# Hybrid pooling and gated-attention block on one core: last down chunk begun in PSUM, mean-square sums taken ahead, squares of the new x held until h2 is split, half of h2 split for all tokens at once

## The chip, the cores and the metric

The kernel runs on one core of a Trainium2 chip. The metric is the device time of one execution in microseconds (us), as the median of three executions. In the names below PE is the matrix engine, ACT the scalar engine, DVE the vector engine, POOL the GpSimd engine and SP the queue that issues most DMAs.

## The reference, cut to what matters

256 tokens of width 2048 go through two mixing branches and a gated feed-forward layer (FFN). The change touches the norms and the FFN; the two branches are left out here.

```python
mixed = (gates[:, :, 0] * y_a + gates[:, :, 1] * y_b) @ w_out[l]
x = x + rms_norm(mixed, norm_mix_post[l])
h = rms_norm(x, norm_ffn_pre[l])
f = (jax.nn.silu(h @ w_ffn_gate[l]) * (h @ w_ffn_up[l])) @ w_ffn_down[l]   # 2048 -> 5632 -> 2048
x = x + rms_norm(f, norm_ffn_post[l])

def rms_norm(x, g):
    y = x * lax.rsqrt(jnp.mean(x * x, axis=-1, keepdims=True) + EPS)
    return y * g
```

## The kernel before, in words

Every product is a job of 512 output columns. A job's weights come in steps of 128x1024 numbers: SP loads `raw` (3 buffers), ACT rounds it to `wh` (`high`, line 316), DVE takes the rest `wl = raw - wh` (`low`, line 320), with 4 buffers of each, and PE multiplies three times for every 128 rows k of the weight and each of the two token tiles t: hi by hi (line 347), hi by lo (348), lo by hi (349), each 128x512 into a bank of PSUM (`acc`). Jobs called fast do part of their rows with fewer products of blocks (class `Part`, lines 362 to 419); they are not changed.

The program is one list of units in the order in which PE is to multiply. `prepare_to` writes the weight work ahead of each unit, `soon` and `bg` hold other work that is put between units. A scheduler then fixes the order in which each engine's instructions stand; each engine goes through its own list in order and waits on semaphores.

Two places matter. The first lies between the last product of the mixing layer (`out`, 3) and the first product of the FFN (`gate`, 0). Its `done` functions call `out_done`: ACT squares the chunk of PSUM with a sum per row (line 821), DVE multiplies by the gain into `mg` (822). After the last chunk `first_residual` sums four partial sums (461), makes the mean plus epsilon (183), POOL raises it to the power -0.5 (185), and `residual_part` makes the new x in four chunks c for each t: `xr` (841). PE transposes it in 128x128 pieces into a bank `tr` (179), ACT writes the high half of h2 (218), DVE the low half (219). `h20h` is the high half of the rows k = 0 to 3 (chunk c = 0), `h21h` those of c = 1, and so on; the gate job takes k = 0 to 7 first for t = 0 (`head=4`), then for t = 1, and then the rest for both. Squares of the new x for the second norm (455) run on ACT between the splits, since all that work lies in one queue `bg`; the norm is needed only when the gate job ends (864).

The second place is the end: the jobs `down` (part, n) add a third of the FFN's rows each into `ff`, on the way out of PSUM (`down_done`, 894 and 896). The last job, (2, 3), does its last four steps for t = 0 and then for t = 1 (`tail=4`). After it come the add (896), the square on ACT (455), the gain (900), the mean (914), POOL's power (916), and `finish`: three chunks of the output on DVE (923) and the fourth by ACT and POOL (920, 921), all sent by SP (926).

Of the kernel before, what the change touches and what calls it, by code (L numbers as in the profile page):

```python
# [100 lines left out]
def tile_hybrid_block(ctx: ExitStack, tc: tile.TileContext, *aps):  # L101
# [79 lines left out]
    def rstd_of(ss, n, width, tag):  # L181
        m = st.tile([P, width], F32, tag="ms", name=nm("ms"))
        dve.tensor_scalar(m, ss, 1.0 / n, EPS, op0=ALU.mult, op1=ALU.add)
        r = one.tile([P, width], F32, tag=tag, name=nm(tag))
        pool.tensor_tensor(r, m, mhalf[:, :width], op=ALU.pow)
        return r
# [72 lines left out]
    class Job:  # L259
# [4 lines left out]
        def __init__(self, w, at, kt, width, fast, lhs, done, across=False, head=0, tail=0):  # L264
            self.w, self.at, self.lhs, self.kt, self.width, self.done = w, at, lhs, kt, width, done
            self.across, self.groups, self.ps, self.extra, self.fast = across, kt // GK, None, None, fast
            both = tuple(range(NT))
# [28 lines left out]
    class Step:  # L296
# [25 lines left out]
        def multiply(self, ts):  # L322
            j, g, hi, lo = self.j, self.g, self.hi, self.lo
            if j.ps is None:
                j.ps = [acc.tile([P, CW], F32, tag="acc", name=nm("acc")) for _ in range(NT)]
                if j.width > CW:
                    j.extra = [bank() for _ in range(NT)]
            for i in range(GK):
                k = g * GK + i
                first, last = k == 0, k == j.kt - 1  # L330
# [9 lines left out]
                for t in ts:  # L340
                    ah, al = j.lhs().get(k, t)
                    out = [(j.ps[t], slice(0, CW))]
                    if j.extra:
                        w = j.width // 2
                        out = [(ps[:, :w], slice(n * w, n * w + w)) for n, ps in enumerate((j.ps[t], j.extra[t]))]
                    for ps, cs in out:
                        pe.matmul(ps, ah, hi[:, i, cs], start=first, stop=False, skip_group_check=j.fast)  # L347
                        pe.matmul(ps, ah, lo[:, i, cs], start=False, stop=False, skip_group_check=j.fast)  # L348
                        pe.matmul(ps, al, hi[:, i, cs], start=False, stop=last, skip_group_check=j.fast)  # L349
# [102 lines left out]
    def squares(src, part, ts, cs):  # L452
        for t in ts:
            for c in cs:
                act.activation(scratch(), src[t][:, c * CW:(c + 1) * CW], AF.Square, accum_out=part[:, t, c:c + 1])

    def total(part, ts, tag):

        w = len(ts)
        ss = st.tile([P, w], F32, tag="ss", name=nm("ss"))  # L460
        dve.tensor_reduce(ss, part[:, ts[0]:ts[0] + w, :], axis=mybir.AxisListType.X, op=ALU.add)
        return rstd_of(ss, D, w, tag)
# [10 lines left out]
    def first_rstd():  # L473
        r = total(part0, (0, 1), "rstd0")
# [227 lines left out]
    def gla_out(h, t, v):  # L702
# [9 lines left out]
        act.activation(scratch(), ps, AF.Square, accum_out=ss)  # L712
        m = st.tile([P, 1], F32, tag="mso", name=nm("mso"))
        r = st.tile([P, 1], F32, tag="rso", name=nm("rso"))
        dve.tensor_scalar(m, ss, 1.0 / DV, EPS, op0=ALU.mult, op1=ALU.add)
        pool.tensor_tensor(r, m, mhalf[:, :1], op=ALU.pow)
# [94 lines left out]
    def out_done(n):  # L811
        def done(j, ts):
# [3 lines left out]
            for t in ts:  # L816
# [4 lines left out]
                act.activation(scratch(), j.ps[t], AF.Square, accum_out=part1[:, t, n:n + 1])  # L821
                dve.tensor_tensor(mg[t][:, c], j.ps[t], bcs[n], op=ALU.mult)
                if n == 3:
                    first_residual(t)
        return done

    def first_residual(t):
        r = total(part1, (t,), f"rstd1{t}")
# [10 lines left out]
    def residual_part(t, c, r):  # L839
        s = slice(c * CW, (c + 1) * CW)  # L840
        dve.scalar_tensor_tensor(xr[t][:, s], mg[t][:, s], r, xr[t][:, s], op0=ALU.mult, op1=ALU.add)
        ps = bank()
        for i in range(4):
            k = c * 4 + i
            v = ps[:, i * P:(i + 1) * P]
            transpose(v, xr[t][:, k * P:(k + 1) * P])
            h2["h"].split(c, (slice(None), i, slice(t * P, (t + 1) * P)), v, scale=column("ffn", k))

    def second_rstd():
        r = total(part2, (0, 1), "rstd2")  # L850
# [5 lines left out]
    fg = {}  # L856
# [28 lines left out]
    def down_done(part, n):  # L885
        def done(j, ts):
# [3 lines left out]
            for t in ts:  # L890
                if ff[t] is None:
                    ff[t] = one.tile([P, D], F32, tag=f"Y{t}", name=f"ff{t}")
                if part == 0:
                    act.activation(ff[t][:, c], j.ps[t], AF.Copy, scale=rz(t, "f"))
                    continue
                dve.scalar_tensor_tensor(ff[t][:, c], j.ps[t], rz(t, "f"), ff[t][:, c], op0=ALU.mult, op1=ALU.add)
                if part == 2:
                    squares(ff, part3, (t,), (n,))
                    fg[t, n] = ff[t][:, c] if n < 3 else scratch()
                    dve.tensor_tensor(fg[t, n], ff[t][:, c], bcs["f", n], op=ALU.mult)  # L900
            if part == 2 and n == 2:

                ss = st.tile([P, NT], F32, tag="ss", name=nm("ss"))
                dve.tensor_reduce(ss, part3[:, :, :3], axis=mybir.AxisListType.X, op=ALU.add)
                rs["3"] = one.tile([P, NT], F32, tag="ms3", name="ms3")
                dve.tensor_scalar(rs["3"], ss, 1.0 / D, EPS, op0=ALU.mult, op1=ALU.add)
            if part == 2 and n == 3:
                for t in ts:
                    finish(t)
        return done  # L910

    def finish(t):
        m = st.tile([P, 1], F32, tag="ms", name=nm("ms"))
        dve.tensor_scalar(m, part3[:, t, 3:], 1.0 / D, rs["3"][:, t:t + 1], op0=ALU.mult, op1=ALU.add)
        r = one.tile([P, 1], F32, tag=f"rstd3{t}", name=f"rstd3{t}")
        pool.tensor_tensor(r, m, mhalf[:, :1], op=ALU.pow)
        for n in (3, 0, 1, 2):
            c = slice(n * CW, (n + 1) * CW)
            if n == 3:
                act.activation(fg[t, n], fg[t, n], AF.Copy, scale=r)  # L920
                pool.tensor_tensor(xr[t][:, c], fg[t, n], xr[t][:, c], op=ALU.add)
            else:
                dve.scalar_tensor_tensor(xr[t][:, c], fg[t, n], r, xr[t][:, c], op0=ALU.mult, op1=ALU.add)
        for n in (0, 1, 3, 2):
            c = slice(n * CW, (n + 1) * CW)
            sync.dma_start(out[0, t * P:(t + 1) * P, c], xr[t][:, c])
# [14 lines left out]
        "down": lambda pn: dict(lhs=lambda: fa[pn[0]], done=down_done(*pn), tail=4 * (pn == (2, 3))),  # L941
# [137 lines left out]
```

## Time and profile before

| | us |
|---|---|
| median of 3 runs | 1502.26 |
| lowest and highest of them | 1500.51, 1502.35 |
| the profiled execution, whole | 1499.66 |
| the span of its instructions | 1497.9 |

The span runs from the first to the last instruction of the profiled execution; the time of the whole execution is 1.76 us longer. Times in the rows below are counted from the start of the span.

### The profile page before, as it was taken

How to read it: one execution, taken by the hardware profiler on the slowest of the kernel's cores; microseconds unless marked ns; L12 is line 12 of the kernel's file. 1: busy time of each engine (PE TensorE's matmuls, PEld its weight loads, DVE VectorE, ACT ScalarE, POOL GpSimd, SP SyncE). 2: the span in 40 equal slices, each digit the busy share in tenths (PEclk: the TensorE clock that was granted, in tenths of full speed). 3: DMA queues.
4: the chain of work that ended last, by engine and by line, in shares of the span. 5: the costliest groups of instructions: out<-in, count | busy, mean ns of one | idle time of the engine just before them, and what ended most of it. 6: DMA issues, size and time to landing. Idle time of an engine off the chain costs nothing.

```text
span 1497.9 us, 23015 instructions
## 1 busy us (share of the span) xinstructions
PE 1481.0 (99%) x8976; PEld 1306.7 (87%) x8976; DVE 1185.1 (79%) x1319; ACT 887.3 (59%) x1150; POOL 64.8 (4%) x91
## 2 busy tenths in 40 slices
PE   9999999999999999999999999999999999999997
PEld 8988999888888888889878989998989888988886
DVE  5755445885578897799768899887889898889996
ACT  6366433555455665556656666666666665666663
POOL 2000000000000000000000000000000000000001
PEclk9999999999999999999999999999999999999999
DMA  9746655345555688558855677767776776677654
GB/s 303 265 160 196 186 186 179 127 128 166 158 174 187 196 250 259 198 169 274 261 184 155 213 223 222 226 215 225 236 217 212 229 225 218 224 232 228 201 176 141
DMA packets 85869, 307.84 MB, mean 206 GB/s; under 512 B 9804, under 2 KB 10016, under 8 KB 85504
## 3 DMA queue, kind: packets, MB, share of 16 engines
q1 hardware_dynamic: 77616, 279.15, 55.6%
q0 software_dynamic: 7440, 25.97, 9.0%
q8 instruction: 70, 1.15, 0.3%
q10 hardware_dynamic: 704, 1.25, 0.3%
q14 instruction: 39, 0.32, 0.1%
HBM read 282.74 MB, written 2.10 MB: 190 GB/s over the span
## 4 chain that ended last, share of the span: by engine, by line
PE 90%; DVE 4%; issue 3%; DMA 2%; ACT 1%; POOL 0%; SPq 0%; DVEq 0%; POOLq 0%; ACTq 0%
PE acc L347 17%; PE acc L349 17%; PE acc L348 17%; PE ac L408 5%; PE ac L407 5%; PE ac L409 5%; PE acc L409 4%; PE acc L407 4%; PE acc L408 4%; PE acc L338 3%; PE acc L336 3%; PE acc L337 3%; PE tr L662 1%; DMA raw<-in_w_in_dram 1%; PE tr L179 1%
## 5 line engine op out<-in xcount | busy, mean ns | idle before, releaser
L316 ACT ACTIVATE wh<-raw 128x1024 fp32r<-128x1024 f32 (+1 forms) x356 | 376.7, 1059 | 360.3 <-PE acc L349 186.3
L320 DVE TENSOR_TENSOR wl<-raw,wh 128x1024 fp32r<-128x1024 f32 (+1 forms) x356 | 435.1, 1224 | 183.1 <-ACT wh L316 181.5
L387 DVE TENSOR_TENSOR wl<-blocks,wh 128x1024 fp32r<-128x1024 f32 x287 | 348.9, 1222 | 73.9 <-ACT wh L383 70.4
L383 ACT ACTIVATE wh<-blocks 128x1024 fp32r<-128x1024 f32 x287 | 301.7, 1058 | 143.3 <-PE acc L349 57.1
L409 PE MATMUL ac<-wh,x 128*128 128x256 f32 x336 | 94.1, 280 | 0.0
L408 PE MATMUL ac<-wl,x 128*128 128x256 f32 x336 | 94.1, 280 | 0.0
L407 PE MATMUL ac<-wh,x 128*128 128x256 f32 x336 | 94.0, 280 | 0.0
L379 POOL DMA_DIRECT2D blocks<-blocks x41 | 35.4, 864 | 811.8 <-DVE wl L320 329.7
L347 PE MATMUL acc<-wh,h22h 128*128 128x512 f32 x176 | 70.3, 399 | 0.2 <-ACT wh L316 0.2
L348 PE MATMUL acc<-wl,h22h 128*128 128x512 f32 x176 | 69.4, 394 | 0.0
L349 PE MATMUL acc<-wh,h23l 128*128 128x512 f32 x176 | 69.4, 394 | 0.0
L347 PE MATMUL acc<-wh,h23h 128*128 128x512 f32 x176 | 69.3, 395 | 0.1
L349 PE MATMUL acc<-wh,h22l 128*128 128x512 f32 x176 | 69.2, 394 | 0.0
L348 PE MATMUL acc<-wl,h23h 128*128 128x512 f32 x176 | 69.1, 393 | 0.0
L407 PEld LDWEIGHTS ac<-wh,x 128*128 128x128 f32 x336 | 63.1, 188 | 2.6
L408 PEld LDWEIGHTS ac<-wl,x 128*128 128x128 f32 x336 | 63.0, 188 | 2.5
L409 PEld LDWEIGHTS ac<-wh,x 128*128 128x128 f32 x336 | 63.6, 189 | 0.0
L372 DVE TENSOR_TENSOR blocks<-blocks,blocks 128x1024 f32<-128x1024 f32 x41 | 50.2, 1224 | 1.1
L368 DVE TENSOR_TENSOR blocks<-blocks,blocks 128x1024 f32<-128x1024 f32 x41 | 50.1, 1222 | 0.9
L347 PE MATMUL acc<-wh,h2h 128*128 128x512 f32 (+1 forms) x128 | 50.3, 393 | 0.0
L370 DVE TENSOR_TENSOR blocks<-blocks 128x1024 f32<-128x1024 f32 x41 | 50.0, 1219 | 0.1
L348 PE MATMUL acc<-wl,h3h 128*128 128x512 f32 (+1 forms) x128 | 49.8, 389 | 0.0
(540 smaller groups left out, 4126.1 us busy)
## 6 DMA issues: line engine op xcount, KB each, us to landing
raw<-in_w_in_dram SPq DMA_DIRECT2D x148, 512.0 KB, 3.6
raw<-in_w_ffn_gate_dram SPq DMA_DIRECT2D x48, 512.0 KB, 4.4
raw<-in_w_ffn_up_dram SPq DMA_DIRECT2D x48, 512.0 KB, 4.7
blocks<-in_w_ffn_down_dram SPq DMA_DIRECT2D x44, 512.0 KB, 4.3
raw<-in_w_ffn_down_dram SPq DMA_DIRECT2D x44, 512.0 KB, 4.4
blocks<-blocks POOLq DMA_DIRECT2D x41, 512.0 KB, 6.0
blocks<-in_w_ffn_gate_dram SPq DMA_DIRECT2D x40, 512.0 KB, 4.3
blocks<-in_w_ffn_up_dram SPq DMA_DIRECT2D x40, 512.0 KB, 4.4
```

The lines of the kernel that those rows point to most:

```text
L316: act.activation(self.hi, self.raw, AF.Copy)
L320: dve.tensor_tensor(self.lo, self.raw, f32(self.hi), op=ALU.subtract)
L347: pe.matmul(ps, ah, hi[:, i, cs], start=first, stop=False, skip_group_check=j.fast)
L348: pe.matmul(ps, ah, lo[:, i, cs], start=False, stop=False, skip_group_check=j.fast)
L349: pe.matmul(ps, al, hi[:, i, cs], start=False, stop=last, skip_group_check=j.fast)
L368: dve.tensor_tensor(b12, b12, b22, op=ALU.add)
L372: dve.tensor_tensor(b21, b21, b12, op=ALU.add)
L383: act.activation(self.hi, self.src, AF.Copy)
L387: dve.tensor_tensor(self.lo, self.src, f32(self.hi), op=ALU.subtract)
L407: pe.matmul(dst, ah, wh, start=i == 0 and p in ("q1", "r5"), stop=False, skip_group_check=True)
L408: pe.matmul(dst, ah, wl, start=False, stop=False, skip_group_check=True)
L409: pe.matmul(dst, al, wh, start=False, stop=i == 3 and p in EARLY, skip_group_check=True)
```

## The change

1. Sums ahead. Squares are scaled so that their sums are means (`scale=D ** -0.5`). `all_but_last` sums the first three chunks of `out` and adds epsilon when the third is done; after the fourth only one addition and the power are left (`power`).
2. Squares of the new x wait for h2. Before each of them DVE copies one number of the last piece of h2 (`h23l`) into the square's scratch tile, so that ACT cannot begin it earlier.
3. Half of h2 is split for all tokens: chunks c = 0 and 1 as before, one t at a time in 128x128 pieces; for c = 2 and 3 a piece holds both t (128x256).
4. The last down chunk begins in PSUM. Column chunk 3 of `ff` is kept without the factor of the norm, ACT copies the sum of the other two parts into the job's PSUM banks before the first product (`begin_last`), and the products add to it. At the end ACT squares straight from PSUM and DVE multiplies by factor and gain in one operation.
5. The end. All output chunks go by DVE, the fourth in two halves of 256 columns; the first half is sent by ACT's queue, the rest by SP's.

```diff
-    def total(part, ts, tag):
+    def power(r, mean, eps):
+        dve.tensor_scalar(m, mean, eps, None, op0=ALU.add)
+        pool.tensor_tensor(r, m, mhalf[:, :w], op=ALU.pow)
+    def all_but_last(part, tag):
+        dve.tensor_reduce(s, part[:, :, :3], axis=mybir.AxisListType.X, op=ALU.add)
+        dve.tensor_scalar(rs[tag], s, EPS, None, op0=ALU.add)
...
-    def squares(src, part, ts, cs):
+    def squares(src, part, ts, cs, behind=None):
         for t in ts:
             for c in cs:
-                act.activation(scratch(), src[t][:, c * CW:(c + 1) * CW], AF.Square, accum_out=part[:, t, c:c + 1])
+                s = scratch()
+                if behind is not None:
+                    dve.tensor_copy(s[:, :1], behind)
+                act.activation(s, src[t][:, c * CW:(c + 1) * CW], AF.Square, scale=D ** -0.5,
+                               accum_out=part[:, t, c:c + 1])
...
     def first_residual(t):
-        r = total(part1, (t,), f"rstd1{t}")
+        power(r, part1[:, t, 3:], rs["1"][:, t:t + 1])
...
-                bg.append(lambda c=c: squares(xr, part2, (0, 1), (c,)))
+                bg.append(lambda c=c: squares(xr, part2, (0, 1), (c,), f32(h2["h"].lo[3][:, 3, T - 1:])))
...
+        ts = (t,) if c < 2 else tuple(range(NT)) if t == NT - 1 else ()
+        w = len(ts) * P
+        for i in range(0, 4 if ts else 0, CW // w if ts else 1):
+            ps = bank()
+            for n in range(CW // w):
+                k = c * 4 + i + n
+                v = ps[:, n * w:(n + 1) * w]
+                for a in ts:
+                    transpose(v[:, (a - ts[0]) * P:(a - ts[0] + 1) * P], xr[a][:, k * P:(k + 1) * P])
+                h2["h"].split(c, (slice(None), i + n, slice(ts[0] * P, (ts[-1] + 1) * P)), v, scale=column("ffn", k))
...
+                if n == 3:
+                    if part == 0:
+                        act.activation(at, j.ps[t], AF.Copy)
+                    elif part == 1:
+                        dve.tensor_tensor(at, j.ps[t], at, op=ALU.add)
+                    else:
+                        act.activation(scratch(), j.ps[t], AF.Square, scale=rs["f/"][:, t:t + 1],
+                                       accum_out=part3[:, t, 3:])
+                        dve.scalar_tensor_tensor(at, j.ps[t], rz(t, "f"), bcs["f", n], op0=ALU.mult, op1=ALU.mult)
+                        finish(t)
+                    continue
...
+    def begin_last(j):
+        for t in range(NT):
+            act.activation(j.ps[t], ff[t][:, 3 * CW:], AF.Copy)
...
-                act.activation(fg[t, n], fg[t, n], AF.Copy, scale=r)
-                pool.tensor_tensor(xr[t][:, c], fg[t, n], xr[t][:, c], op=ALU.add)
...
+        for n, (a, w) in enumerate(((0, CW), (CW, CW), (2 * CW, CW), (3 * CW, CW // 2), (3 * CW + CW // 2, CW // 2))):
+            c = slice(a, a + w)
+            dve.scalar_tensor_tensor(xr[t][:, c], ff[t][:, c], r, xr[t][:, c], op0=ALU.mult, op1=ALU.add)
+            (act if n == 3 else sync).dma_start(out[0, t * P:(t + 1) * P, c], xr[t][:, c])
```

The order in which the engines' instructions stand moves with it. On ACT, from the last weight rounding before h2 on, the kernel before has these rows (L821 squares the last chunk of `out` for t = 1, L455 the new x; `tr` is the bank of PSUM that a piece is split from):

```order
L218 ACTIVATE h20h<-tr_7117,cols 128x128
L821 ACTIVATE scr_7168,part_120<-acc_6979 128x512
L218 ACTIVATE h21h<-tr_7143,cols 128x128
L218 ACTIVATE h20h<-tr_7117,cols 128x128
L316 ACTIVATE wh_7179<-raw_7177 128x1024
L455 ACTIVATE scr_7326,part_121<-xr_6622 128x512
L218 ACTIVATE h20h<-tr_7117,cols 128x128
L218 ACTIVATE h21h<-tr_7143,cols 128x128
```

The changed kernel has these at the same place:

```order
L218 ACTIVATE h20h<-tr_7119,cols 128x128
L218 ACTIVATE h21h<-tr_7145,cols 128x128
L835 ACTIVATE scr_7170,part_120<-acc_6983 128x512
L218 ACTIVATE h20h<-tr_7119,cols 128x128
L318 ACTIVATE wh_7179<-raw_7177 128x1024
L218 ACTIVATE h21h<-tr_7145,cols 128x128
L218 ACTIVATE h20h<-tr_7119,cols 128x128
```

The square in front of the third piece of h20 is gone; one split has moved ahead of the square of `out`. The eight squares of the new x now stand together on ACT between the weights of the next job, `up` 0 (wh_7361 is its first step, wh_7385 its second):

```order
L318 ACTIVATE wh_7361<-raw_7359 128x1024
L463 ACTIVATE scr_7310,part_121<-xr_6622 128x512
L463 ACTIVATE scr_7313,part_121<-xr_6628 128x512
L463 ACTIVATE scr_7328,part_121<-xr_6622 128x512
L463 ACTIVATE scr_7331,part_121<-xr_6628 128x512
L463 ACTIVATE scr_7352,part_121<-xr_6622 128x512
L463 ACTIVATE scr_7355,part_121<-xr_6628 128x512
L463 ACTIVATE scr_7377,part_121<-xr_6622 128x512
L463 ACTIVATE scr_7380,part_121<-xr_6628 128x512
L318 ACTIVATE wh_7385<-raw_7383 128x1024
L318 ACTIVATE wh_7411<-raw_7409 128x1024
L887 ACT_TABLE_LOAD
```

Before, three of the eight stood this late, one by one, between the last splits and the weights. On DVE the sum of those squares (L469) and what follows it stand in front of the low half of the second step, wl_7387, as they now read:

```order
L322 TENSOR_TENSOR wl_7363<-raw_7359,wh_7361 128x1024
L462 COPY scr_7377<-h23l 128x1
L462 COPY scr_7380<-h23l 128x1
L469 TENSOR_REDUCE ss_7401<-part_121 128x2
L185 TENSOR_SCALAR ms_7404<-ss_7401 128x2
L874 TENSOR_SCALAR rstd2s<-rstd_1143_7403 128x2
L322 TENSOR_TENSOR wl_7387<-raw_7383,wh_7385 128x1024
```

Before, the sum stood between the low halves of the last gate step and the first `up` step, and nothing waited for POOL's power there. At the end, DVE's rows for t = 1 were these before:

```order
L896 SCALAR_TENSOR_TENSOR ff_9241<-acc_14245,rstd_1147_7413,ff_9241 128x512
L900 TENSOR_TENSOR scr_14353<-ff_9241,bc_14306 128x512
L914 TENSOR_SCALAR ms_14355<-part_122,ms_14236 128x1
L923 SCALAR_TENSOR_TENSOR xr_6628<-ff_9241,rstd_14357,xr_6628 128x512 x3
L1074 UNCONDITIONAL_BRANCH
```

In the changed kernel they are these:

```order
L927 SCALAR_TENSOR_TENSOR ff_9235<-acc_14239,rstd_1143_7403,bc_14302 128x512
L185 TENSOR_SCALAR ms_14349<-part_122,ms_14230 128x1
L950 SCALAR_TENSOR_TENSOR xr_6628<-ff_9235,rstd_14348,xr_6628 128x512 x3
L950 SCALAR_TENSOR_TENSOR xr_6628<-ff_9235,rstd_14348,xr_6628 128x256 x2
L1100 UNCONDITIONAL_BRANCH
```

One 128x512 operation on DVE is gone and two of 128x256 are added; ACT's square now reads PSUM and stands ahead of DVE's first row instead of behind it, and POOL keeps only the power.

## Rows read from the trace of the kernel before

**Rows 1.** The profile's page, part 1: busy time, share of span, instructions.

```profile
PE 1481.0 (99%) x8976; PEld 1306.7 (87%) x8976; DVE 1185.1 (79%) x1319; ACT 887.3 (59%) x1150; POOL 64.8 (4%) x91
```

**Rows 2.** Windows: length; busy us of PE, PEld, DVE, ACT, POOL; PEclk, DMA share, GB/s.

```profile
770.00:802.00 32.00, 30.24 (x139) 22.43 (x140) 26.18 (x55) 24.74 (x60) 2.29 (x3) 1.00 0.48 156
802.00:1000.00 198.00, 198.00 (x1227) 176.71 (x1226) 178.33 (x186) 129.40 (x163) 6.90 (x8) 1.00 0.68 209
1400.00:1471.00 71.00, 69.42 (x444) 61.83 (x443) 68.99 (x76) 46.36 (x65) 2.83 (x4) 1.00 0.59 186
```

**Rows 3.** Timeline of PE, gate 0: start, duration, operation, [idle before, releaser].

```profile
769.41 0.40 PE L349 MATMUL acc<-wh,m3l 128*128 128x512 f32 x1
770.19 0.33 PE L179 MATMUL tr<-ident,xr 128*128 128x128 f32 x1 [0.38 <-DVE xr L841]
...
775.03 0.50 PE L347 MATMUL acc<-wh,h20h 128*128 128x512 f32 x1 [0.62 <-ACT h20h L218]
...
781.13 0.48 PE L347 MATMUL acc<-wh,h20h 128*128 128x512 f32 x1
...
788.32 0.27 PE L179 MATMUL tr<-ident,xr 128*128 128x128 f32 x1
...
788.66 0.27 PE L179 MATMUL tr<-ident,xr 128*128 128x128 f32 x1
...
800.81 0.39 PE L349 MATMUL acc<-wh,h23l 128*128 128x512 f32 x1
801.04 0.39 PE L347 MATMUL acc<-wh,h20h 128*128 128x512 f32 x1
```

**Rows 4.** Groups by line, 764 to 802: busy us, mean ns, idle before.

```profile
L320 DVE TENSOR_TENSOR wl<-raw,wh 128x1024 fp32r<-128x1024 f32 x11 | 13.4, 1221 | 6.4 <-ACT wh L316 6.4
L455 ACT ACTIVATE scr<-xr 128x512 f32<-128x512 f32 x8 | 5.2, 650 | 0.2 <-DVE xr L841 0.2
```

**Rows 5.** Timeline of DVE and of ACT around gate 0.

```profile
768.37 0.14 DVE L461 TENSOR_REDUCE ss<-part 128x1 f32<-128x4 f32 x1
773.99 0.63 ACT L455 ACTIVATE scr<-xr 128x512 f32<-128x512 f32 x1
774.60 0.37 ACT L218 ACTIVATE h20h<-tr,cols 128x128 fp32r<-128x128 f32 x1
799.84 1.06 ACT L316 ACTIVATE wh<-raw 128x1024 fp32r<-128x1024 f32 x1 [2.20 <-DMA raw<-in_w_ffn_up_dram]
```

**Rows 6.** Line 219: duration ns (min/median/max), first and last start, forms.

```profile
L219 DVE SCALAR_TENSOR_TENSOR h20l<-tr,cols,h20h x8: 344/346/353, 771.9 to 785.5; 128x128 fp32r<-128x128 f32 x8
L219 DVE SCALAR_TENSOR_TENSOR h0l<-tr,cols,h0h x4: 474/480/485, 7.2 to 10.1; 128x256 fp32r<-128x256 f32 x4
```

**Rows 7.** Timeline: ACT's rounding before the last job, PE's first row of it.

```profile
1464.00 1.05 ACT L316 ACTIVATE wh<-raw 128x1024 fp32r<-128x1024 f32 x1
1471.24 0.40 PE L347 MATMUL acc<-wh,f20h 128*128 128x512 f32 x1
```

**Rows 8.** Timeline of DVE, POOL and SP at the end, line 923, DMA landing.

```profile
1488.25 0.75 DVE L896 SCALAR_TENSOR_TENSOR ff<-acc,rstd,ff 128x512 f32<-128x512 f32 x1
1490.67 3.08 DVE L923 SCALAR_TENSOR_TENSOR xr<-ff,rstd,xr 128x512 f32<-128x512 f32 x3 [0.66 <-POOL rstd L916]
L923 DVE SCALAR_TENSOR_TENSOR xr<-ff,rstd,xr x6: 747/753/1783, 1485.1 to 1492.0; 128x512 f32<-128x512 f32 x6
1491.46 1.74 POOL L921 TENSOR_TENSOR xr<-scr,xr 128x512 f32<-128x512 f32 x1 [0.83 <-ACT scr L920]
DMA to landing us min/median/max: 2.2/2.3/2.4
1494.10:1495.50 1.40, 0.00 (x0) 0.00 (x0) 0.00 (x0) 0.00 (x0) 0.00 (x0) 0.50 0.97 364
```

**Rows 9.** Timeline of ACT and DVE around the square of `out`, chunk 3.

```profile
767.04 0.60 ACT L821 ACTIVATE scr<-acc 128x512 f32<-128x512 f32 x1 [3.15 <-PE acc L349]
767.76 0.69 DVE L822 TENSOR_TENSOR mg<-acc,bc 128x512 f32<-128x512 f32 x1 [2.62 <-ACT scr L821]
```

More of the change, by code (lines that the diff above doesn't have):

```diff
@@ L179, in transpose @@
         pe.transpose(dst, src, ident[:src.shape[0], :src.shape[0]])
[L181 to L186, printed above, removed]
+    def power(r, mean, eps):
+        w = mean.shape[-1]
+        m = st.tile([P, w], F32, tag="ms", name=nm("ms"))
+        dve.tensor_scalar(m, mean, eps, None, op0=ALU.add)
+        pool.tensor_tensor(r, m, mhalf[:, :w], op=ALU.pow)
     def extra(a):
@@ L327, in multiply @@
                     j.extra = [bank() for _ in range(NT)]
+                if j.begin:
+                    j.begin(j)
             for i in range(GK):
                 k = g * GK + i
-                first, last = k == 0, k == j.kt - 1
+                first, last, loose = k == 0 and not j.begin, k == j.kt - 1, j.fast or j.begin is not None
                 if j.across:
@@ L346, in multiply @@
                     for ps, cs in out:
-                        pe.matmul(ps, ah, hi[:, i, cs], start=first, stop=False, skip_group_check=j.fast)
-                        pe.matmul(ps, ah, lo[:, i, cs], start=False, stop=False, skip_group_check=j.fast)
-                        pe.matmul(ps, al, hi[:, i, cs], start=False, stop=last, skip_group_check=j.fast)
+                        pe.matmul(ps, ah, hi[:, i, cs], start=first, stop=False, skip_group_check=loose)
+                        pe.matmul(ps, ah, lo[:, i, cs], start=False, stop=False, skip_group_check=loose)
+                        pe.matmul(ps, al, hi[:, i, cs], start=False, stop=last, skip_group_check=loose)
     pending = deque()
@@ L450, in tile_hybrid_block, with total @@
     part0 = one.tile([P, NT, 4], F32, tag="part0", name="part0")
-    def squares(src, part, ts, cs):
+    def squares(src, part, ts, cs, behind=None):
         for t in ts:
             for c in cs:
-                act.activation(scratch(), src[t][:, c * CW:(c + 1) * CW], AF.Square, accum_out=part[:, t, c:c + 1])
-    def total(part, ts, tag):
[L459 to L462, printed above, removed]
+                s = scratch()
[3 more added lines that the diff above has]
+                               accum_out=part[:, t, c:c + 1])
+    def total(part, tag):
+        ss = st.tile([P, NT], F32, tag="ss", name=nm("ss"))
+        dve.tensor_reduce(ss, part, axis=mybir.AxisListType.X, op=ALU.add)
+        r = one.tile([P, NT], F32, tag=tag, name=nm(tag))
+        power(r, ss, EPS)
+        return r
+    def all_but_last(part, tag):
+        s = st.tile([P, NT], F32, tag="ss", name=nm("ss"))
+        dve.tensor_reduce(s, part[:, :, :3], axis=mybir.AxisListType.X, op=ALU.add)
+        rs[tag] = one.tile([P, NT], F32, tag=f"ms{tag}", name=f"ms{tag}")
+        dve.tensor_scalar(rs[tag], s, EPS, None, op0=ALU.add)
     def along(r, tag):
@@ L473, in first_rstd @@
     def first_rstd():
-        r = total(part0, (0, 1), "rstd0")
+        r = total(part0, "rstd0")
         rs["z"] = [r[:, t:t + 1] for t in range(NT)]
@@ L841, in residual_part @@
         dve.scalar_tensor_tensor(xr[t][:, s], mg[t][:, s], r, xr[t][:, s], op0=ALU.mult, op1=ALU.add)
[L842 to L847, printed above, removed]
+        ts = (t,) if c < 2 else tuple(range(NT)) if t == NT - 1 else ()
[8 more added lines that the diff above has]
+                h2["h"].split(c, (slice(None), i + n, slice(ts[0] * P, (ts[-1] + 1) * P)), v, scale=column("ffn", k))
     def second_rstd():
-        r = total(part2, (0, 1), "rstd2")
+        r = total(part2, "rstd2")
+        rs["f/"] = one.tile([P, NT], F32, tag="rstd2s", name="rstd2s")
+        dve.tensor_scalar(rs["f/"], r, D ** -0.5, None, op0=ALU.mult)
         rs["f"] = [r[:, t:t + 1] for t in range(NT)]
@@ L855, in tile_hybrid_block @@
     fa = {}
-    fg = {}
     ff = [None] * NT
@@ L901, in done @@
             if part == 2 and n == 2:
[L903 to L909, printed above, removed]
-        return done
+                all_but_last(part3, "3")
@@ L940, in tile_hybrid_block @@
         "up": lambda m: dict(lhs=lambda: h2["h"], done=ffn_up_done(m)),
-        "down": lambda pn: dict(lhs=lambda: fa[pn[0]], done=down_done(*pn), tail=4 * (pn == (2, 3))),
+        "down": lambda pn: dict(lhs=lambda: fa[pn[0]], done=down_done(*pn), tail=4 * (pn == (2, 3)),
+                             begin=begin_last if pn == (2, 3) else None),
     }
```

34 lines of the change are left out of this document (13 added, 21 removed).

## The prediction

> **What bounds the kernel now.** The page's first part comes first: PE is busy for 1481.0 of 1497.9 us [rows 1], so time can only be won where PE waits or where its work has ended. The windows say where: from 802 to 1000 PE has no gap, while from 770 to 802 it is idle for 1.76 us and from 1400 to 1471 for 1.58 [rows 2]; DVE is at 68.99 of 71 us in the last of these. PEclk reads 1.00 in all three, the upper of its two levels (2.4 GHz), so the clock is no term here. After the last product, at 1488.2, nothing of PE remains, and 9.7 us go by until the end of the span.
>
> Busy time hides part of the waits, because matmuls overlap. So I read the timeline of PE through gate 0 and counted. A 128x512 product starts 0.23 us after the one before it (800.81, 801.04) and a transpose put in between adds 0.11 (788.32 to 788.66 holds one of each, 0.34) [rows 3]. From 769.41 to 801.04, which is 31.63 us, start 103 products and 32 transposes: 103 x 0.233 + 32 x 0.11 = 27.5 us. So 4.1 us are waits, all of it in the stretch that the change rewrites. That is the most that edits 1 to 3 can give.
>
> What sets these waits is a chain per piece of h2: transpose, ACT's high half (0.37), DVE's low half (0.35), and only then the next transpose into the same bank [rows 3, 5, 6]. With three handovers of about 0.04 that is some 1.1 us per row k, against 3 x 0.233 + 2 x 0.11 = 0.9 us of PE's work for it. So PE waits a little at each of the first rows even if nothing stands in between, and more when a square (0.61 us from 773.99 to 774.60 [rows 5]) or a weight (DVE 1.22 [rows 4]) does.
>
> **Sums ahead (edit 1).** The reduction of 0.14 us leaves the path between the gain and the power [rows 5], and the first transpose, which waited for the new x [rows 3], comes some 0.15 us earlier. The reduction that is added after chunk 2 lies under PE's products there. The same edit in the eight attention heads keeps the number of operations: nothing.
>
> **Squares later, half of h2 in wide pieces (edits 2 and 3).** I followed the changed order with the durations of these rows. The third row k waited 0.62 us for a split behind a rounding and a square [rows 3, 5]; without the square about 0.4 is left of it. The rows up to k = 7 of t = 0 then end so that t = 1 begins at 780.1 instead of 781.13 [rows 3], 1.0 earlier, though four transposes fewer have been done by then (0.44). The waits that I find are 0.4 us at the first transpose, 0.35, 0.75 and 0.5 around the second to fourth row of t = 0, and 0.2, 0.4, 0.3, 0.1 and 0.2 in t = 1; nearly all come from the same chain, the last from the low half of the fifth weight, which comes just behind the splits. Together they are 3.1 us against 4.1 (rounded): **1.0 us is won**. The wide pieces cost ACT and DVE less (DVE 0.48 for 256 columns against 2 x 0.35 [rows 6]), 8 times 0.2 us on each; PE needs them only in rows k from 8 on, so this shortens a queue and no path. The bounds are nothing (the chain fills what the squares leave) and 4.1 us; I take 1.0, which is near the lower end, because the chain of 1.1 against 0.9 stays.
>
> The eight squares now take 8 x 0.61 = 4.9 us of ACT in one piece, after the last piece of h2 (at about 791.7 by the same count) and after the first `up` weight (to about 793). They end at about 798, POOL's power near 799, and the norm is needed when gate 0 ends, at 800.0. Behind them stands the second `up` weight: 1.06 on ACT and 1.22 on DVE, so ready at 800.2; PE asks for it one step of 12 products after gate 0, at 802.8. That is 2.6 us of cover. If it is gone, each further microsecond is paid. The eight copies of one number have no row of their kind: between nothing and 0.14 us each (the nearest narrow operation, the reduction), at most 1.1 us of DVE, which waits 6.4 us for ACT's roundings in this stretch [rows 4]. The last of those before gate 0's end waited 2.20 us for its transfer [rows 5]; that transfer is asked for when a low half frees its buffer, and the low halves come 1.5 to 2 us earlier now.
>
> **Begin in PSUM (edit 4).** Two ACT copies of 128x512 join the queue before the last job. No row shows one that goes from SBUF to PSUM; a 128x128 split takes 0.37 and a 128x1024 rounding 1.05, the 128x512 square 0.65 [rows 4, 5, 7], which I take: 1.3 us. They stand behind the rounding that ends at 1465.05, and PE starts the job at 1471.24 [rows 7], so 4.9 us hide them. The plain copy and add in parts 0 and 1 cost what the scaled ones did: nothing.
>
> **The end (edits 4 and 5).** Before, from 1488.25 to the first output operation at 1490.67 are 2.42 us [rows 8]: add, square, mean, power. Now square and the combined multiply stand there in the other order. ACT's square of PSUM holds DVE for 0.72 (767.04 to 767.76 [rows 9]), and DVE's operation takes the 0.75 of the old add; the mean follows on DVE without a change of engine. That is 0 to 0.2 shorter: 0.1.
>
> Then come the outputs. Three of them took 3.08 us [rows 8], though five of the six in line 923 take about 0.75 and begin 0.66 apart; the sixth took 1.78, with POOL's addition (1491.46, 1.74) running beside it. With POOL's addition gone three take 2.07. The two halves, at 256 columns, take up to 0.48 each with a step of 0.40 (DVE [rows 6]), so the last ends 2.8 us after the first begins: 0.3 earlier than 3.08. The last transfer is half as long: 512 KB moved in 1.40 us [rows 8], so 0.35 less for 128 KB, and it landed 2.3 us after its issue. As the transfers follow one another closely, I count 0.2 of it. Sum: 0.1 + 0.3 + 0.2 = **0.6 us**, with bounds of 0.2 and 1.0.
>
> ACT's queue sends the first half of t = 0 ahead of the square of t = 1. That half is ready 2.3 + 2.5 = 4.8 us after PE's last product for t = 0, and the square is due 24 x 0.233 = 5.6 us after it: 0.8 us hide the sending; past that it is paid.
>
> What made the sixth output operation take 1.78 us? The page GPSIMD Engine Reference of the Trainium skill, section 1 (Specifications), says that GpSimd's way to SBUF is shared with the vector engine and contended by vector instructions with two inputs in SBUF. By this the 1.03 us go with POOL's addition, as counted. If instead the output transfers that run at that time slow DVE, they stay, and the end becomes 0.4 us longer instead of 0.6 shorter. The trace speaks for the page: the only long one overlaps POOL.
>
> **Sum.** 1499.66 - 1.0 - 0.6 = 1498.1 for the profiled execution. That one lies 2.6 us under the median of the runs, 1502.26, whose runs spread from 1500.51; so for the median 1502.26 - 1.6 = **1500.6**. Less than 0.2% (3.0 us) can hardly be told from no change.
>
> **Rivals.**
>
> *All waits of gate 0 go.* If a bank's next transpose in fact follows sooner than I count, or the order lets the other banks fill in, all 4.1 us are won: 1502.26 - 4.1 - 0.6 = 1497.6. For it: the longest wait, 0.62 us, ends on ACT [rows 3], which loses the squares. Against: the chain of 1.1 us. With everything that passes 3.0 us in total, 0.18.
>
> *The lead is given back.* In 1400 to 1471 DVE is busy 97% [rows 2]. If that stretch's end is set by DVE work that does not move with PE, the 1.0 us is lost and only the end remains: 1501.7. Against it: the work there is released by PE's own products, and PE has no gap from 802 to 1000. 0.14.
>
> *The end is longer.* If the output transfers were what slowed DVE, the end adds 0.4, and the sum is 1502.26 - 1.0 + 0.4 = 1501.7. 0.05.
>
> *Slower: the squares block the `up` weights.* Place: the second `up` step, behind eight squares on ACT and behind their sum and POOL's power on DVE. It decides once the squares begin more than 2.6 us later than 793, for instance because the first `up` weight's transfer is late, as the third's was (2.20 [rows 5]). With all 4.9 us of squares exposed: 1502.26 - 1.6 + 4.9 = 1505.6. Against: the transfers are asked for earlier. 0.07. The page PSUM — Partial Sum Buffer of the Trainium skill, section Engine vs sequencer instructions, calls these engines' queues strict FIFO, so that a weight could not pass the squares; no row of the trace shows an instruction that passes another.
>
> **How the numbers follow.** The forecast has 0.56. The range takes in the rival at 1497.6 and, upward, the lead and the end lost together, with the spread of the runs (about 1 us either way): 1497.6 to 1503.0. The slower rival lies outside. Faster by over 0.2%: the first rival and a part of the forecast's spread, 0.22; slower by over 0.2%: 0.07; within: 0.71.
>
> **What would show it.** Gate 0: no square between the splits; t = 1 starting about 10.5 us after PE's product at 769.41, and the first `up` product 30.6 us after it. The squares should be over about 2 us before gate 0's last product, with no wait of PE for `wl` at the second `up` step. At the last job's start PE should not wait for ACT's copies. At the end, three output operations should take 2.07 us and the last transfer be asked for 0.4 us sooner after PE's last product. Wrong would be: PE waiting at the `up` steps, a long output operation without POOL beside it, or waits in gate 0 that go almost wholly.

## The result, and the profile after

The changed kernel takes 1505.44 us (median of 9 runs, 1504.17 to 1507.54) against 1500.51 us of the kernel before in the same set of runs. The ratio is 1.0029, with a 95% interval of 1.002 to 1.0038: slower by about 5 us, where 1.6 us faster was forecast. The profiled execution has a span of 1502.7 us, 4.8 more than before.

The page's first part of the changed kernel shows where to look:

```profile
PE 1485.8 (99%) x8976; PEld 1312.3 (87%) x8976; DVE 1184.0 (79%) x1322; ACT 885.8 (59%) x1142; POOL 61.4 (4%) x89
```

PE does the same 8976 operations as before and is busy for 4.8 us more [rows 1]. So the loss is not idle time of PE: as the rows below show, the products themselves take longer. The windows of the changed kernel that answer to the first two of [rows 2], 2.66 us later, which is about half a microsecond or less off the same places of the program:

```profile
772.66:804.66 32.00, 30.85 (x141) 22.91 (x142) 25.66 (x55) 24.05 (x53) 2.40 (x3) 1.00 0.45 140
804.66:1002.66 198.00, 198.00 (x1223) 177.12 (x1222) 178.44 (x185) 128.91 (x162) 6.90 (x8) 1.00 0.67 211
```

In the first, PE is busy for 0.61 us more than before, so it waits less in gate 0. In the second it has no gap in either kernel, but it does 1223 operations in the time of 1227. The granted clock is 1.00 in both. A stretch with nothing but products of 256 columns shows this best: the 768 products in a row of the jobs called `across`, which the change does not touch. Windows of 80 us inside it, of the kernel before and then of the changed one:

```profile
162.00:242.00 80.00, 80.00 (x685) 80.00 (x684) 40.67 (x38) 30.04 (x29) 0.00 (x0) 1.00 0.61 189
```

```profile
162.00:242.00 80.00, 80.00 (x674) 80.00 (x673) 40.24 (x38) 29.67 (x28) 0.00 (x0) 1.00 0.59 185
```

PE is busy for all 80 us in both and does 11 products fewer. In the changed kernel's timeline this stretch begins and ends with these rows:

```profile
159.50 0.28 PE L340 MATMUL acc<-h0h,wh 128*128 128x256 f32 x1
...
250.89 0.28 PE L342 MATMUL acc<-h3l,wh 128*128 128x256 f32 x1
```

That is 91.39 us for 767 steps, 119.2 ns each; before it was 117.1.

The timeline of PE through gate 0 and at the last product, the rows that answer to [rows 3]:

```profile
772.07 0.39 PE L353 MATMUL acc<-wh,m3l 128*128 128x512 f32 x1
772.72 0.33 PE L179 MATMUL tr<-ident,xr 128*128 128x128 f32 x1 [0.26 <-DVE xr L859]
...
782.97 0.50 PE L351 MATMUL acc<-wh,h20h 128*128 128x512 f32 x1
...
803.05 0.40 PE L353 MATMUL acc<-wh,h23l 128*128 128x512 f32 x1
803.29 0.39 PE L351 MATMUL acc<-wh,h20h 128*128 128x512 f32 x1
...
1476.68 0.40 PE L351 MATMUL acc<-wh,f20h 128*128 128x512 f32 x1
...
1493.29 0.40 PE L353 MATMUL acc<-wh,f22l 128*128 128x512 f32 x1
```

From the last product before the first transpose of the new x to the first product of `up` it is 803.29 - 772.07 = 31.22 us, against 31.63 [rows 3]. From the last product, 1493.29, to the end of the span it is 9.41; before it was 10.04, by its last product's row in the timeline of PE:

```profile
1487.82 0.40 PE L349 MATMUL acc<-wh,f22l 128*128 128x512 f32 x1
```

The table cuts each span at the same five products; columns are us. "To 256s" ends where the 768 products begin, "gate 0" is the stretch just given, "FFN" goes from the first product of `up` to the last of all, "end" from there to the end of the span. The first two rows are the kernel before and the changed one, the others most of the experiments below (names with b_ are the kernel before in another layout, all others the changed one).

| kernel | to 256s | 768 of 256 | to gate 0 | gate 0 | FFN | end | span |
|---|---|---|---|---|---|---|---|
| before | 158.28 | 89.82 | 521.31 | 31.63 | 686.77 | 10.04 | 1497.85 |
| changed | 159.50 | 91.39 | 521.18 | 31.22 | 690.00 | 9.41 | 1502.70 |
| a_pad64 | 159.40 | 89.83 | 522.26 | 31.23 | 686.95 | 9.45 | 1499.12 |
| b_pad64 | 158.30 | 91.39 | 521.84 | 31.64 | 690.56 | 10.03 | 1503.77 |
| b_al | 158.29 | 87.05 | 518.83 | 31.70 | 684.45 | 10.06 | 1490.38 |
| a_al | 157.47 | 87.05 | 519.12 | 31.30 | 683.76 | 9.43 | 1488.13 |
| s_sq | 158.20 | 87.05 | 519.74 | 31.50 | 683.83 | 9.41 | 1489.73 |
| s_nar | 156.89 | 87.05 | 518.84 | 31.89 | 683.70 | 9.40 | 1487.77 |
| s_pool | 157.76 | 87.05 | 519.17 | 31.28 | 683.70 | 10.21 | 1489.16 |
| a_256 | 157.62 | 86.95 | 515.22 | 31.24 | 680.25 | 9.40 | 1480.68 |

Between before and changed, the loss is 1.57 us in the 768 products, 3.23 in the FFN and 1.22 at the start; gate 0 and the end win 0.41 and 0.63. The first column, where PE waits for the first transfers, differs by up to 1.4 us between the kernels with the layout of a_al alone (156.89 to 158.29), and against the kernel with equal addresses and without the edits it is 1.1 and 1.2 us more in a_pad64 and the changed kernel and 0.8 less in a_al. I take it for no part of the change; no run tests that.

### The profile page after: what moved, and what is told of

Read it like the earlier page. It is cut to its first block, busy times and chain, and to the rows that moved or that the text cites. A ratio compares the mean times of both kernels' runs of the same rounds, so it can differ in the third digit from the quotient of the medians.

```text
span 1502.7 us, 23012 instructions
## 1 busy us (share of the span) xinstructions
PE 1485.8 (99%) x8976; PEld 1312.3 (87%) x8976; DVE 1184.0 (79%) x1322; ACT 885.8 (59%) x1142; POOL 61.4 (4%) x89
## 4 chain that ended last, share of the span: by engine, by line
PE 91%; DVE 3%; issue 2%; DMA 2%; ACT 1%; SPq 0%; POOL 0%; DVEq 0%; POOLq 0%; ACTq 0%
PE acc L351 18%; PE acc L353 18%; PE acc L352 18%; PE ac L412 5%; PE ac L413 5%; PE ac L411 5%; PE acc L411 4%; PE acc L413 4%; PE acc L412 4%; PE acc L342 3%; PE acc L340 3%; PE acc L341 3%; PE tr L678 1%; PE tr L179 1%; DMA raw<-in_w_in_dram 1%
## 5 line engine op out<-in xcount | busy, mean ns | idle before, releaser
L351 PE MATMUL acc<-wh,h3h 128*128 128x512 f32 (+1 forms) x128 | 49.9, 390 | 0.0
```

## The experiments

**The theory.** The change adds two small tiles (`ms1`, `rstd2s`, each taking 32 bytes of every partition) ahead of the weight tiles `raw`, `wh` and `wl`, and takes the tile `mso` away behind them. The built program has a list of where each tile lies; by it `wh` and `wl` begin at 96 modulo 128 bytes before and at 32 after, 64 further on, while `h`, `x`, `h2` and `f`, which meet them in the products, stay where they were. No view of the profile shows addresses. The theory is that this move makes the products slower, and the rivals that the edits themselves do (another order, another program length), or the start. Of a product's two operands, the *stationary* one below is the 128x128 block that PE loads as the weight (PEld), and the *moving* one is that with the 256 or 512 columns; `wh` and `wl` are stationary in the `across` jobs and moving in the others. *Distance* is the start of the moving operand less that of the stationary one, in bytes of a partition, modulo 128 unless said otherwise. A *step* is the time from the start of one product to that of the next of the same width, taken from all of a trace; those over 150 ns (256 columns) and 260 ns (512) are left out of the means as waits.

**1 and 2. The addresses swapped.** b_pad64 is the kernel before and a_pad64 the changed one; in each the last small tile ahead of the weights is 64 bytes longer. No engine's list of instructions changes.

```diff
-        r = one.tile([P, 1], F32, tag=f"rstd3{t}", name=f"rstd3{t}")
+        r = one.tile([P, 1 + 16 * t], F32, tag=f"rstd3{t}", name=f"rstd3{t}")[:, :1]
```

Expected of b_pad64: 

> The kernel before with one small tile made 64 bytes longer, so that raw, wh, wl, scr and blocks lie 64 bytes further on, where they lie in the changed kernel (seen modulo 128); no instruction is added or moved. Address theory (256-column products cost 1.5 ns more at the new addresses, 4385 of them in the trace: 6.5 us): 1500.5 + 6.5 = 1507, and the mean step from one 256-column product to the next goes from 117.3 to 118.8 ns. Rival, the edits themselves slow PE (other order, other program length): 1500.5 and 117.3 ns, as before. Rival, the first 60 us (transfers of x) make the loss: 1500.5 as well.

Expected of a_pad64: 

> The changed kernel with the same 64 bytes, which puts raw, wh, wl, blocks and fx back where they lie before, seen modulo 128. Address theory: 1505.4 - 6.5 = 1499, with a step of 117.3 ns between 256-column products; it would then be about 1.5 us faster than the kernel before, as forecast. Rivals (the edits slow PE; the first 60 us): 1505.4 and 118.8 ns, no change.

Measured: b_pad64 takes 1505.55 us, 1.0034 of the kernel before (1.0021 to 1.0046); a_pad64 takes 1500.20, ratio 0.9997 (0.9988 to 1.0006). The mean steps of 256 columns are 118.8 and 117.3 ns, where the changed kernel and the one before have 118.8 and 117.3. The window with nothing but these products, first of b_pad64, then of a_pad64:

```profile
162.00:242.00 80.00, 80.00 (x674) 80.00 (x673) 39.89 (x37) 29.61 (x29) 0.00 (x0) 1.00 0.56 185
```

```profile
162.00:242.00 80.00, 80.00 (x686) 80.00 (x685) 40.23 (x38) 30.58 (x29) 0.00 (x0) 1.00 0.56 186
```

The 64 bytes alone make the kernel before as slow as the changed one, and take the loss from the changed one. The rivals fall.

**3 and 4. Two other places.** a_pad32 and a_pad96 are the changed kernel with 8 * t and 24 * t in that line.

Expected of a_pad32: 

> The changed kernel with 32 bytes more: wh then begins at 64 modulo 128 instead of 32. Address theory: another step than 118.8 ns, not known which; bounds 113 (the shortest step that a kind of 256-column products shows before) to 120 ns, so 1480 to 1510. Rivals: 1505.4, 118.8 ns.

Expected of a_pad96: 

> The changed kernel with 96 bytes more: wh then begins at 0 modulo 128. Address theory: another step than 118.8 ns, bounds as for 32 bytes: 1480 to 1510. Rivals: 1505.4, 118.8 ns.

Measured: 1497.16 us (0.9975, 0.9965 to 0.9985) and 1502.99 (1.0019, 1.0010 to 1.0028), with steps of 116.8 and 118.9 ns. So each of the four places has its own time, and one of them beats both kernels. Sorted by distance, the 256-column steps of the four traces (before, changed and these two) are 119.1 ns at 0, 117.5 at 32, 115.8 at 64 and 119.0 at 96, with some 3800 to 5800 steps each; each of these means is over several kinds of products. This gave the theory that the distance decides.

**5 to 8. The distance made the same everywhere.** Small tiles are made longer until `wh` and `wl` lie at 64 modulo 128 and all that meets them at 0 (a_al, and b_al from the kernel before), all at 0 (a_same), or the reverse of the first (a_rev). The diff is that of a_al.

```diff
-    part0 = one.tile([P, NT, 4], F32, tag="part0", name="part0")
+    part0 = one.tile([P, NT + 6, 4], F32, tag="part0", name="part0")[:, :NT]
-                u = st.tile([P, HW], F32, tag="u", name=nm("u"), bufs=2)
+                u = st.tile([P, HW + 8], F32, tag="u", name=nm("u"), bufs=2)[:, :HW]
-        r = one.tile([P, 1], F32, tag=f"rstd3{t}", name=f"rstd3{t}")
+        r = one.tile([P, 1 + 16 * t], F32, tag=f"rstd3{t}", name=f"rstd3{t}")[:, :1]
```

Expected of a_al: 

> The changed kernel with small tiles made longer, so that wh and wl lie at 64 modulo 128 and every operand that meets them in a product (h, x, fx, f, o, m, h2) at 0. Distance theory (what counts is how far the two operands of a product lie apart modulo 128): from the earlier traces, distance 64 gives steps of 116.2 ns for 256 columns (118.8 in the changed kernel, 4385 of them) and 231.4 ns for 512 columns (233.8, 3392 of them), so 1505.4 - 11.4 - 8.1 = 1486; up to 1492 if VectorE becomes the bound where it is 97% busy. Rival, only the place of the weight tiles counts: as with 32 bytes more, 1497.

Expected of b_al: 

> The kernel before with the same layout as a_al. Distance theory: 1500.5 less (117.3 - 116.2) x 4385 and (234.1 - 231.4) x 3392 = 4.8 + 9.2, so 1486.5. What the edits themselves are worth is the difference to a_al: 1.6 us by the prediction (a_al faster); about 0.1 by the pair with equal addresses that has been run.

Expected of a_same: 

> The changed kernel with all of these tiles at 0 modulo 128, distance 0. Distance theory: 119.1 ns for 256 columns (slower by 1.3 us in all), 230.9 ns for 512 columns (faster by 9.8 us): 1497. Rival, only the place of the weight tiles counts: as with 96 bytes more, 1503.

Expected of a_rev: 

> The layout of a_al turned round: wh and wl at 0 modulo 128, what meets them at 64. Distance theory: as a_al, 1486 to 1492. Rival, only the place of the weight tiles counts: 1503, as with 96 bytes more.

Measured: a_al 1490.72 us (0.9934, 0.9922 to 0.9947), b_al 1491.54 (0.9938, 0.9926 to 0.9951), a_same 1501.42 (1.0007, 0.9998 to 1.0015), a_rev 1490.95 (0.9931, 0.9917 to 0.9944). Steps are 116.0 and 231.3 ns in a_al, 116.1 and 231.3 in a_rev, 119.0 and 231.0 in a_same. Turning the layout round changes nothing, so it is the distance and not the place of the weights: the rival's 1503 is 12 us off. The window of a_al, then of a_rev:

```profile
162.00:242.00 80.00, 80.00 (x708) 80.00 (x707) 41.76 (x39) 30.81 (x29) 0.00 (x0) 1.00 0.62 197
```

```profile
162.00:242.00 80.00, 80.00 (x708) 80.00 (x707) 42.05 (x39) 30.81 (x29) 0.00 (x0) 1.00 0.62 196
```

Each is 34 products more than the changed kernel does in the same 80 us; a_same does 674, as that does. All four lie 4 to 5 us above the time that the distances gave by my count, for one reason: I had taken the 512-column step of the changed kernel as 233.8 ns, a mean with waits in it. Without them it is 232.4, so a_al gains 2.8 ns x 4380 + 1.1 ns x 3341 = 15.9 us (measured 14.7), and a_same loses 1.2 (0.28 ns before rounding) and gains 4.7, 3.5 in all (measured 4.0).

**9. The same for 256 bytes.** In a_al the 512-column steps are 229.8 ns where the distance modulo 256 is 64 and 232.8 where it is 192, half of them each, because the buffers of a weight tile lie 4224 bytes apart, an odd multiple of 128. a_256 has them 4352 apart and all 512-column products at 64.

```diff
-            self.hi = wp.tile([P, GK, self.j.width], F32R, tag="wh", name=nm("wh"))
+            self.hi = wp.tile([P, GK * max(self.j.width, 544 * (self.j.width > CW))], F32R, tag="wh", name=nm("wh"))[:, :GK * self.j.width].rearrange("p (g c) -> p g c", g=GK)
```

The same is done for `wl`; `part0`, `part1` and the last small tile are made longer again, and the two tiles `rows` share the room of `x`.

Expected: 

> The changed kernel in the layout of a_al, and beyond it the buffers of wh and wl lie a multiple of 256 bytes apart (4352 instead of 4224), h, h2, f, o and m at 0 modulo 256 and all of wh and wl at 64; two small tiles share the room of x. Distance theory, carried from modulo 128 to modulo 256: in a_al the 512-column products took 229.8 ns a step at distance 64 modulo 256 and 232.9 at 192, half of them each, so all at 64 is 1.5 ns less for 3400 of them, 5.2 us: 1490.7 - 5.2 = 1485.5. Rival, only the distance modulo 128 counts and the two means differ for another reason (which buffer, which job): 1490.7.

Measured: 1482.38 us, ratio 0.9875 (0.9856 to 0.9895), steps of 115.2 and 229.4 ns. It is the fastest version: 19 us under the kernel before in the same set of runs, and 23 under the changed one. It gains 3 us more than expected: the 256-column products with `x`, whose distance modulo 256 is now 192 throughout, became quicker too, which I had not counted (117.7 to 115.3 ns for `ac` from `wh` and `x`). In its timeline the FFN stretch is 1471.28 - 791.03 = 680.25 us:

```profile
791.03 0.39 PE L351 MATMUL acc<-wh,h20h 128*128 128x512 f32 x1
...
1471.28 0.39 PE L353 MATMUL acc<-wh,f22l 128*128 128x512 f32 x1
```

**10 and 11. Which edit won the time in gate 0.** At equal addresses gate 0 wins 0.40 to 0.42 us (three pairs of the table). s_sq and s_nar undo edits 2 and 3, each alone, in the layout of a_al.

```diff
-                bg.append(lambda c=c: squares(xr, part2, (0, 1), (c,), f32(h2["h"].lo[3][:, 3, T - 1:])))
+                bg.append(lambda c=c: squares(xr, part2, (0, 1), (c,)))
```

```diff
-        ts = (t,) if c < 2 else tuple(range(NT)) if t == NT - 1 else ()
+        ts = (t,)
```

Expected of s_sq: 

> The layout of a_al, with the squares of the new x not held until h2 is split (edit 2 undone). From the last product of out to the first of up it was 29.1 us in a_al and 29.6 in the kernel before with that layout. If the squares between the splits were the wait that the change took away (the prediction's step): 29.4 to 29.6. If the wide pieces did it, or the sums ahead: 29.1, no longer than a_al. In the median neither can be told: 1490.7 to 1491.2.

Expected of s_nar: 

> The layout of a_al, with all four chunks of h2 split one token tile at a time in 128x128 pieces (edit 3 undone). By the prediction the wide pieces shorten a queue and no path: 29.1 us from the last product of out to the first of up, as in a_al. Rival, the wide pieces are what the stretch gained: 29.4 to 29.6. In the median neither can be told: 1490.7 to 1491.2.

Measured: 1491.31 us (0.9935, 0.9917 to 0.9952) and 1490.60 (0.9933, 0.9917 to 0.9949), which tells nothing, as expected. The expectations count from the last product of `out`, 2.2 us behind the mark of the table; the differences to a_al are the same either way. Without holding the squares gate 0 is 0.20 us longer, without the wide pieces 0.59. By the count of the expectations that is 29.3 and 29.7: the first lies between its two cases, the second just above its rival. Each rests on one trace. Two traces of the changed gate 0 in one layout agree to 0.02 us (a_al, s_pool), but over all layouts of the changed kernel it is 31.22 to 31.43, so the 0.20 holds for this layout alone. In the timeline of s_nar the stretch is 794.67 - 762.78 = 31.89 us:

```profile
762.78 0.39 PE L353 MATMUL acc<-wh,m3l 128*128 128x512 f32 x1
...
794.67 0.39 PE L351 MATMUL acc<-wh,h20h 128*128 128x512 f32 x1
```

That is longer than with all edits undone (b_al, 31.70). The wide pieces are on the path, then, and held squares without them win nothing. Which wait of PE they shorten is not shown.

**12. POOL's addition beside the outputs.** s_pool is a_al with an addition on POOL for each token tile at the end.

```diff
         power(r, part3[:, t, 3:], rs["3"][:, t:t + 1])
+        pool.tensor_tensor(scratch(), ff[t][:, :CW], ff[t][:, CW:2 * CW], op=ALU.add)
```

Expected: 

> The layout of a_al, and behind each of the two last powers POOL adds two 128x512 chunks of ff into a scratch tile that nothing reads, so that POOL works in SBUF beside the output operations again, as before the change; the output transfers stay as they are. The five output operations of the last token tile took 2.87 us without POOL's addition (3.08 for three with it, one of them 1.78). If POOL's addition held DVE: about 1.0 more, 3.9, and the time from the last product to the end 9.4 + 1.0 = 10.4 us. Rival, the transfers or the one long operation's data made it long: 2.9 and 9.4.

Measured: 1491.12 us (0.9939, 0.9923 to 0.9956). The order put the addition for t = 1 far ahead, at 1466.77, so only that of t = 0 lies beside output operations, and both cases stand in one timeline. The second row is the first of the five operations in the third, from a window that holds it alone:

```profile
1476.15 1.29 POOL L948 TENSOR_TENSOR scr<-ff 128x512 f32<-128x512 f32 x1
1476.21 1.79 DVE L951 SCALAR_TENSOR_TENSOR xr<-ff,rstd,xr 128x512 f32<-128x512 f32 x1 [0.68 <-POOL rstd L186]
1476.21 3.91 DVE L951 SCALAR_TENSOR_TENSOR xr<-ff,rstd,xr 128x512 f32<-128x512 f32 x5 [0.68 <-POOL rstd L186]
1480.17 0.69 ACT L925 ACTIVATE scr<-acc,rstd2s 128x512 f32<-128x512 f32 x1 [5.55 <-DVE xr L951]
1482.52 2.87 DVE L951 SCALAR_TENSOR_TENSOR xr<-ff,rstd,xr 128x512 f32<-128x512 f32 x5 [0.66 <-POOL rstd L186]
```

The window of the long operation:

```profile
1476.21:1478.00 1.79, 1.79 (x9) 1.49 (x8) 1.79 (x2) 0.00 (x0) 1.23 (x1) 1.00 0.00 0
```

Five operations take 3.91 us with POOL beside them and 2.87 without. The addition costs DVE 1.04 us, all of it in the one operation of 1.79. No transfer ran while it did (DMA share 0.00), and the five of t = 1 took 2.87 with transfers under way (share 0.44), so the transfers are not the cause. The kernel before has two such operations, not one, as the timelines of POOL and of DVE show:

```profile
1485.88 1.76 POOL L921 TENSOR_TENSOR xr<-scr,xr 128x512 f32<-128x512 f32 x1 [0.84 <-ACT scr L920]
1486.41 1.78 DVE L923 SCALAR_TENSOR_TENSOR xr<-ff,rstd,xr 128x512 f32<-128x512 f32 x1
...
1492.00 1.75 DVE L923 SCALAR_TENSOR_TENSOR xr<-ff,rstd,xr 128x512 f32<-128x512 f32 x1
```

Each began while POOL added, the second beside the addition at 1491.46 [rows 8], and in all three cases DVE's operation ends 0.55 to 0.56 us after POOL's (1478.00 and 1477.44 in s_pool). That would fit an operation that is held until POOL's has ended; but the three overlaps are nearly alike (1.20 to 1.23 us), so they do not show whether the price is fixed. The end became 0.78 us longer, though by another way than expected: ACT's queue sends half a chunk of t = 0 before it squares t = 1, so the square waits for t = 0's outputs and begins 1.21 us after the last product (1478.96) instead of 0.43.

## Why the prediction was wrong

**The step that failed** is the first: "PE is busy for 1481.0 of 1497.9 us [rows 1], so time can only be won where PE waits or where its work has ended". It takes the busy time as fixed. The sum therefore had terms for the edits alone and none for 4380 products of 256 columns in jobs that the change does not touch; these became 1.5 ns longer, 6.6 us, and 3340 of 512 columns 0.2 ns shorter, 0.7 us. With the 1.0 us that the edits win that makes 1500.51 + 4.9 = 1505.4, where 1505.44 was measured. That it fits so closely is luck: this count puts all 5.9 us of the loss into the products, the table only 4.7 and the rest into the start, and for b_pad64 the same count comes out 0.4 us too high. No rival had this cause; the slower one blamed the squares. A smaller fault is the base: 1502.26, the median of three runs, lies 1.75 us above that of nine, 1500.51, so the forecast of a kernel 1.6 us faster meant 1498.9.

**Sums ahead** held: the first transpose comes 0.65 us after the product ahead of it (772.07, 772.72) instead of 0.78 [rows 3], and 0.68 instead of 0.82 in a_al and b_al, for a forecast of 0.15.

**Squares later and wide pieces** were mis-sized: 1.0 us forecast for all of gate 0, 0.41 measured. (The waits listed there add up to 3.2, not 3.1, and its own 780.1 puts the second token tile 10.7 us after the mark, not 10.5.) The second token tile began 10.9 us after the mark (782.97), 0.82 earlier than before, and the first product of `up` 31.2 instead of 30.6: half of the lead was lost again in between. Of the forecast 1.0 only 0.2 depends on the squares. And "this shortens a queue and no path" was wrong: the wide pieces are worth 0.59 when the squares are held.

**The cover of the squares** held. The timeline of ACT, and then that of DVE, at the end of gate 0 in the changed kernel:

```profile
796.20 0.62 ACT L463 ACTIVATE scr<-xr 128x512 f32<-128x512 f32 x1
...
800.50 0.62 ACT L463 ACTIVATE scr<-xr 128x512 f32<-128x512 f32 x1
...
801.11 1.99 ACT L318 ACTIVATE wh<-raw 128x1024 fp32r<-128x1024 f32 x2
```

```profile
795.93 0.46 DVE L462 COPY scr<-h23l 128x1 f32<-128x1 f32 x6
...
802.49 2.36 DVE L322 TENSOR_TENSOR wl<-raw,wh 128x1024 fp32r<-128x1024 f32 x2
```

Eight squares take 4.9 us in one piece and end 1.9 us before the gate's last product (803.05). The second `up` step is ready at about 803.7, the first half of that last row, and PE asks for it 12 products after 803.29, at 806.0: 2.3 us of cover against 2.6 forecast. The slower rival did not come about. The copies take under 0.08 us each.

**Begin in PSUM** held. The two copies are done 5.2 us before PE's first row of the last job (1476.68), and cost 1.10 us where 1.3 was taken. The timeline of ACT:

```profile
1470.42 1.10 ACT L943 ACTIVATE acc<-ff 128x512 f32<-128x512 f32 x2
```

**The end** held: 0.63 us won for a forecast of 0.6. The rows of ACT and DVE that answer to [rows 8]:

```profile
1493.72 0.69 ACT L925 ACTIVATE scr<-acc,rstd2s 128x512 f32<-128x512 f32 x1 [4.83 <-PE acc L353]
...
1494.53 0.75 DVE L927 SCALAR_TENSOR_TENSOR ff<-acc,rstd,bc 128x512 f32<-128x512 f32 x1 [1.19 <-ACT scr L925]
...
1496.06 2.87 DVE L950 SCALAR_TENSOR_TENSOR xr<-ff,rstd,xr 128x512 f32<-128x512 f32 x5 [0.66 <-POOL rstd L186]
```

The first output begins 2.77 us after the last product's start instead of 2.85 (0.08, forecast 0.1), the outputs take 2.87 instead of 3.08 (0.21, forecast 0.3), and the rest, 0.34, lies behind the last output operation and is put down to the shorter last transfer (forecast 0.2). (The prediction's own terms, 3 x 0.66 + 0.40 + 0.48, make 2.86 for the outputs, so its 0.3 should have been 0.2.) The prediction read one long operation among the six of line 923; there are two, each beside an addition of POOL's, so its conclusion stands. That POOL's addition, and not the transfers, made them long is shown by s_pool. The rule of the Trainium skill on this (GPSIMD Engine Reference, section 1, Specifications) agrees with it. The 0.8 us that was said to hide the sending on ACT's queue was there: in s_pool outputs that took 1.04 us longer made the square 0.78 us late.

**The lead given back** cannot be told at its size: at equal addresses the FFN stretch of the changed kernel is 0.18 us longer in one pair and 0.56 and 0.69 shorter in the two others.

What the edits are worth is 0.40 + 0.6 = 1.0 us by the traces of each pair. The medians of the pairs (the second across two sets of runs) differ by 0.13, 0.11 and 0.82 us in the same direction, which with intervals of over 1 us either way neither confirms nor contradicts it.

## What to carry to other kernels

A tile of a few bytes moves every tile that is allocated behind it, and here that alone was worth 5 us, five times what the edits did. Where a change adds or removes small tiles, compare an untouched stretch in which the engine is never idle: if the number of operations in a window of the same length differs, the cause is not in the reordered work, and a pair of kernels with the tiles padded back to their places tells the two apart. Once this is seen it is worth more than the change: the layout with the best distances is 1.25% faster than the kernel before.

## What the runs showed of the hardware that I had not expected

The time from one product to the next on TensorE depends on how far its two operands lie apart in a partition of SBUF, at a granted clock of 1.00 (2.4 GHz) and with no wait in the trace. For the 768 products of 256 columns in a row it is 119.2 ns at distance 0 and at 96, 117.1 at 32 and 113.3 to 113.5 at 64. For 512 columns it is 231.0 at 0, 233.5 at 32, 233.4 at 96 and 231.3 at 64, and at 0 and 64 the distance modulo 256 matters too: 229.4 at 0 and 232.7 at 128 (a_same), 229.8 at 64 and 232.8 at 192 (a_al). Why that is so, for instance a resource that both reads of SBUF share, no run shows; only that swapping the places of the two operands leaves it unchanged (a_rev).

The Trainium skill (TensorE: Matmul & The Clock Gate, section Step-by-step: what each phase is for) says that TensorE has two independent read ports of SBUF and that loading the next weights takes no read bandwidth from the running matmul. Taken to hold wherever the operands lie, their place would not matter and the changed kernel would have taken about 1499.5. The measurements differ from it, by 5.7 ns of 119.2 in the clearest stretch, and they decide.
